# A two-layer trunk on one core: q's second part over zeros, slots moved, last squares added to the fold

## The chip, the cores and the metric

The kernel runs on one core of a Trainium2 chip. A core has TensorE (PE) for matrix products, fed by its own weight loads (PEld), VectorE (DVE), ScalarE (ACT), GpSimd (POOL), SyncE (SP) and 16 DMA engines that they share. The metric is the time of one execution on the device, in microseconds. Before the change it is 965.36 us, the median of three runs (965.27 to 965.42).

## What is computed

A trunk of two layers for 256 tokens of width 1024, in float32. Each layer adds half an FFN, a mixer, and half an FFN, each on a normed input; a last norm follows. The mixer of layer 0 has eight attention heads of width 64, where the three dilated windows come down to one causal score matrix with a fixed mask, and beside them four groups of a spatial gate. The mixer of layer 1 is causal attention with 16 heads of width 64 (with 256 tokens there is one block of 256, so no past block is chosen).

```python
def swiglu(x, w_gate, w_up, w_down):
    return (jax.nn.silu(x @ w_gate) * (x @ w_up)) @ w_down
...
    for layer in range(DEPTH):
        h = h + 0.5 * swiglu(rms_norm(h, ffn1_norm[layer]), ...)
        hn = rms_norm(h, mix_norm[layer])
        if layer % 2 == 0:
            h = h + ab_mixer(hn, ...)
        else:
            h = h + c_mixer(hn, ...)
        h = h + 0.5 * swiglu(rms_norm(h, ffn2_norm[layer]), ...)
    return rms_norm(h, final_norm)
```

In a head: scores are q times k over 64, masked, softmax by rows, then times v.

## The kernel before

Every float32 product is made of three products of rounded parts: each operand is split into a first part, rounded to the format that TensorE takes at full rate (`F32R`), and a second part, the rest. `mm3` (L224 to L226) adds first x first, first x second and second x first. Splitting is an ACT copy that rounds and a DVE subtraction; for the weights these are L105 and L106, elsewhere L229 and L230.

The weights come as a stream of 1 MB tiles: SP loads them into three raw buffers, ACT and DVE split them, and four split buffers are ahead of TensorE. The activations lie transposed, with the width on the 128 partitions, so that a projection tile is 24 products of 128x128 weights by 256 columns (`tile_of`). Two heads of 64 make one tile of 128 partitions, a pair.

Scores need only 64 rows a head. To have q first x (k first + k second) in one product, the 128 rows hold the head's k first on its own half and k second on the other half (`put_k`, tiles k0 and k1), and q first twice (`put_q`, tile q). The remaining product, q second x k first, has the 64 rows of the head alone (`kh` and `ql[r]`, L665). So in `scores` a product with 128 rows (L664) and one with 64 rows (L665) take turns, twice for each head. `put_q` rounds the pair to q1 on ACT, subtracts on DVE into ql, and copies q1 four times on POOL. `put_k` rounds on ACT and subtracts on POOL (L651, L652). In the first mixer put_q and put_k first scale the bank by the norm's row (`scaled`, tile qk); in the second, `rows=True`, only put_k does.

After the scores, DVE adds the mask and takes the row extreme (L668), ACT makes the exponentials (L671), DVE the reciprocal (L674), ACT (first mixer, L678) or POOL (second, L680) scales. `turn` transposes the probabilities on TensorE (L688) and splits them into pth and ptl; `weighted` multiplies them by v and splits the result into mix, which `project` uses.

Around the projection tiles, `Slots` counts a step after each tile (24 products, 8 x 3 in `project`), and calls what is listed for that step: scores, turn, weighted, in the first mixer also mixing (the spatial products L829, which need vn, the normed gate, and wsT) and turn_spatial. That list sets where TensorE does this work; on each of the other engines the framework's scheduler fixes an order when the program is built, and each engine runs its list in that order. Only the first stage has an order written by hand.

The norm's sums are collected as the residual is finished: `Next.pair` is called for four pairs of tiles, squares each on ACT (L279) and adds it on DVE to acc (L283, 128x512). `sums`, later in the next stage, folds acc's two halves into one (L287, 128x256), has TensorE sum over partitions (L290, tile ones), and POOL takes the root (L233). `spread` turns that root to a row through TensorE (L308).

The tiles of a mixer live in a pool that takes the memory of the FFN before it.

Of the kernel before, what the change touches and what calls it, by code (L numbers as in the profile page):

```python
# [10 lines left out]
F32 = mybir.dt.float32  # L11
F32R = mybir.dt.float32r
AF = mybir.ActivationFunctionType
ALU = mybir.AluOpType

S = 256
# [15 lines left out]
LINE, SHIFT = 64, 16  # L32
# [110 lines left out]
def trunk(ctx: ExitStack, tc: tile.TileContext, a, out):  # L143
    nc = tc.nc
# [11 lines left out]
    def bank():  # L156
        return ps.tile([128, 512], F32, name="bank")
# [65 lines left out]
    def mm3(p, sh, sl, mh, ml, start, stop):  # L223
        nc.tensor.matmul(p, sh, mh, start=start, stop=False)  # L224
        nc.tensor.matmul(p, sh, ml, start=False, stop=False)  # L225
        nc.tensor.matmul(p, sl, mh, start=False, stop=stop)  # L226

    def split(hi, lo, src):
        nc.scalar.activation(hi, src, AF.Copy)  # L229
        nc.vector.tensor_sub(lo, src, hi.bitcast(F32))  # L230
# [8 lines left out]
    def both(t):  # L239
        return t.rearrange("p (j s) -> p j s", j=2)  # L240

    def twice(v):
        return v.unsqueeze(1).to_broadcast([128, 2, S])

    class Next:
# [19 lines left out]
        def pair(self, i, p, row=None, pool=None):  # L265

            xs = X[:, 2 * i : 2 * i + 2, :]
            if row is None:
                nc.vector.tensor_add(xs, both(p), xs)
            else:  # L270
                t = pool.tile([128, 2, S], F32, name="part")
                nc.vector.tensor_mul(t, both(p), twice(row))
                nc.vector.tensor_add(xs, t, xs)
            for k in (2 * i, 2 * i + 1):
                self.hi(k, X[:, k])
            for k in (2 * i, 2 * i + 1):
                self.lo(k, X[:, k])
            q = wk.tile([128, 2, S], F32, name="sq" if i else "acc", bufs=1)
            nc.scalar.activation(q, xs, AF.Square, scale=1.0 / math.sqrt(D))  # L279
            if i == 0:  # L280
                self.acc = q
            else:
                nc.vector.tensor_add(self.acc, self.acc, q)  # L283

        def sums(self):
            f = self.acc[:, 0]
            nc.vector.tensor_add(f, f, self.acc[:, 1])  # L287
            p = bank()
            for t in range(NT):
                nc.tensor.matmul(p[:, t : t + 1], f[:, t * 128 : (t + 1) * 128], ones[:, :1], start=True, stop=True)  # L290
            m = wk.tile([128, NT], F32, name="ms")
            nc.vector.tensor_scalar(m, p[:, :NT], EPS, None, op0=ALU.add)  # L292
            self.root(m)
# [322 lines left out]
    def make_attention(mp, mask_cols, nheads, v, mix, engine, rows=False):  # L616

        qs, ks, probs, pts = {}, {}, {}, {}
        pairs, flying = (4, 5) if rows else (3, 4)
        mask = mp.tile([128, 384], F32, name="mask")  # L620
        nc.scalar.dma_start(mask, a["consts"][:, mask_cols])

        def scaled(bk):
            t = mp.tile([128, S], F32, name="qk", bufs=pairs - 1)
            nc.vector.tensor_mul(t, bk[:, :S], norm["row"])
            return t

        def sides(j):
            return slice(j * 64, j * 64 + 64), slice(64 - j * 64, 128 - j * 64)

        def put_q(p, bk):

            t = bk[:, :S] if rows else scaled(bk)
            q1 = mp.tile([128, S], F32R, name="q1", bufs=2)
            ql = mp.tile([128, S + LINE], F32R, name="ql", bufs=pairs)[:, SHIFT : SHIFT + S]
            qq = mp.tile([128, 2 * S + LINE], F32R, name="q", bufs=pairs)
            split(q1, ql, t)
            for j in range(2):
                q = qq[:, SHIFT + j * S : SHIFT + (j + 1) * S]
                r, o = sides(j)  # L640
                for to in (r, o):
                    nc.gpsimd.tensor_copy(q[to, :], q1[r, :].bitcast(F32))  # L642
                qs[2 * p + j] = (q, ql[r, :])

        def put_k(p, bk):

            t = scaled(bk)
            for j in range(2):
                k = mp.tile([128, S], F32R, name=f"k{j}", bufs=pairs)
                r, o = sides(j)  # L650
                nc.scalar.activation(k[r, :], t[r, :], AF.Copy)  # L651
                nc.gpsimd.tensor_sub(k[o, :], t[r, :], k[r, :].bitcast(F32))  # L652
                ks[2 * p + j] = (k, k[r, :])

        def scores(h):
            q, ql = qs.pop(h)
            k, kh = ks.pop(h)
            sc = bank()
            pr = mp.tile([128, 384], F32, name="pr", bufs=flying)
            nm = wk.tile([128, 2], F32, name="nm")  # L660
            l = wk.tile([128, 2], F32, name="l")
            for b in range(2):
                bs = slice(b * 128, b * 128 + 128)
                nc.tensor.matmul(sc[:, b * S : (b + 1) * S], q[:, bs], k, start=True, stop=False)  # L664
                nc.tensor.matmul(sc[:, b * S : (b + 1) * S], ql[:, bs], kh, start=False, stop=True)  # L665
            for b, (c0, n) in enumerate(((0, 128), (128, 256))):
                cs = slice(c0, c0 + n)
                nc.vector.tensor_tensor_reduce(pr[:, cs], sc[:, b * S : b * S + n], mask[:, cs],  # L668
                                               norm["score"][:, b : b + 1] if rows else -SCALE, 3e38,
                                               op0=ALU.add, op1=ALU.min, accum_out=nm[:, b : b + 1])  # L670
                nc.scalar.activation(pr[:, cs], pr[:, cs], AF.Exp, bias=nm[:, b : b + 1], scale=-1.0,  # L671
                                     accum_out=l[:, b : b + 1])
            rl = wk.tile([128, 2], F32, name="rl")
            nc.vector.reciprocal(rl, l)  # L674
            for b, (c0, n) in enumerate(((0, 128), (128, 256))):
                cs = slice(c0, c0 + n)
                if engine is nc.scalar:
                    nc.scalar.activation(pr[:, cs], pr[:, cs], AF.Copy, scale=rl[:, b : b + 1])  # L678
                else:
                    engine.tensor_scalar(pr[:, cs], pr[:, cs], rl[:, b : b + 1], None, op0=ALU.mult)  # L680
            probs[h] = pr

        def turn(h):
            p, j = divmod(h, 2)
            pr = probs.pop(h)
            tp = bank()
            for i in range(3):
                nc.tensor.transpose(tp[:, i * 128 : (i + 1) * 128], pr[:, i * 128 : (i + 1) * 128], ident)  # L688
            if j == 0:
                pts[p] = [mp.tile([128, 2, 384], F32R, name=n, bufs=2) for n in ("pth", "ptl")]  # L690
            split(pts[p][0][:, j, :], pts[p][1][:, j, :], tp[:, :384])

        def weighted(p):
            o = bank().rearrange("p (j c) -> p j c", j=2)
            pth, ptl = pts.pop(p)
            vs = slice(p * 128, (p + 1) * 128)
            mm3(o, v[0][:, 0, vs], v[1][:, 0, vs], pth[:, :, :256], ptl[:, :, :256], True, False)
            mm3(o[:, :, 128:], v[0][:, 1, vs], v[1][:, 1, vs], pth[:, :, 256:], ptl[:, :, 256:], False, True)
            for j in range(2):
                r = slice(j * 64, j * 64 + 64)  # L700
                split(mix[0][r, p], mix[1][r, p], o[r, j, :].rearrange("p (t c) -> p t c", t=NT))

        return put_q, put_k, scores, turn, weighted
# [82 lines left out]
    def ab_mixer(phase):  # L786
        with tc.tile_pool(name="mp", bufs=1) as mp:
# [4 lines left out]
            put_q, put_k, scores, turn, weighted = make_attention(mp, slice(0, 384), 8, v, mix, nc.scalar)  # L792
# [9 lines left out]
            def turn_spatial():  # L802
                pw = bank()
                for g in range(4):
                    nc.tensor.transpose(pw[:, g * 128 : (g + 1) * 128], wsp[:, g, :], ident)
                nc.vector.tensor_copy(wsT, pw.rearrange("p (g c) -> p g c", g=4))
                nc.gpsimd.affine_select(wsT, wsT, pattern=[[0, 4], [1, 128]], compare_op=ALU.is_ge, fill=0.0,
                                        base=0, channel_multiplier=-1)
# [28 lines left out]

            slots = Slots()
            slots.at((9,), lambda _: turn_spatial())
            slots.at((14, 15, 16, 17), mixing)  # L840
            slots.at((5, 6, 7, 8, 20, 20, 21, 21), scores)
            slots.at((8, 9, 10, 11, 22, 22, 23, 23), turn)
            slots.at((11, 13, 24, 25), weighted)

            def put_u(i, p):
                nc.vector.tensor_mul(uT[:, i, :], p[:, :S], norm["row"])
# [81 lines left out]
```

## Time and profile before

| | |
|---|---|
| median of three runs | 965.36 us |
| the profiled execution | 965.54 us |
| its span, first to last instruction | 963.8 us |
| mean granted clock of TensorE | 0.998 |
| first mixer, about | 190 to 290 us |
| second mixer, about | 652 to 774 us |

A group of the profile reads: line, engine, operation, out <- in by the program's names, partitions x elements, count | busy time in us, mean ns of one | idle time of the engine before them, and what ended it. A row of the timeline reads: start in us, duration in us, engine, line, operation, tiles, count of merged instructions, and in brackets the idle time before it with what ended it. PE rows are products, PEld rows their weight loads; both run as a pipeline, so that the duration of one is longer than the distance to the next. Lines of `split` and `mm3` are those of the helper, so the tile's name tells whose they are.

### The profile page before, as it was taken

Reading aid. Unit: us, or ns where it says so; the run is one execution under the profiler, and the core shown is the slowest. Engines: PE = TensorE matmul, PEld = TensorE weight load, DVE = VectorE, ACT = ScalarE, POOL = GpSimd, SP = SyncE. Lnnn points to the kernel's source line nnn. Section 1 sums busy time; section 2 is a strip of 40 time slices with the busy share of each in tenths; the row PEclk is TensorE's granted clock in tenths of the full one; section 3 lists DMA queues with packets and bytes.
Section 4 is the critical chain, followed back from the end, with each engine's and each line's share of the span. In section 5 each row is a group of like instructions: output and inputs, shape, how many; then the busy total and the mean of one; then the engine's idle time right before and its main releaser. Section 6 shows DMA issues by size and latency. Waiting matters only on the chain.

```text
span 963.8 us, 18092 instructions
## 1 busy us (share of the span) xinstructions
PE 952.8 (99%) x7679; PEld 916.9 (95%) x7679; DVE 599.3 (62%) x848; ACT 502.2 (52%) x789; POOL 88.2 (9%) x122
## 2 busy tenths in 40 slices
PE   9999999999999999999999999999999999999997
PEld 8999999978999999999999999998979999999886
DVE  6866556656867665655666565656767676566543
ACT  7744445457675544444454453446666566454431
POOL 0000000030400000000000000004665200000000
PEclk9999999999999999999999999999999999999999
DMA  9865555655445656556666665565434465565521
GB/s 295 276 205 187 186 186 178 218 193 175 132 132 181 208 181 204 180 175 205 202 195 199 185 197 169 193 219 184 139 125 131 132 198 179 181 210 179 208 96 44
DMA packets 153537, 174.86 MB, mean 181 GB/s; under 512 B 3008, under 2 KB 142192, under 8 KB 153456
## 3 DMA queue, kind: packets, MB, share of 16 engines
q1 hardware_dynamic: 151888, 171.54, 55.8%
q10 hardware_dynamic: 1568, 2.17, 0.7%
q8 instruction: 60, 0.98, 0.4%
q14 instruction: 21, 0.17, 0.0%
HBM read 172.65 MB, written 1.05 MB: 180 GB/s over the span
## 4 chain that ended last, share of the span: by engine, by line
PE 94%; DVE 2%; issue 1%; ACT 1%; DMA 1%; POOL 0%; SPq 0%; POOLq 0%
PE bank L224 28%; PE bank L225 28%; PE bank L226 28%; PE bank L539 2%; PE bank L542 2%; PE bank L538 2%; PE bank L665 2%; DVE wlo L106 1%; PE bank L664 1%; PE bank L688 1%; DMA raw<-in_ffn_w_gate 1%; DVE xTl L262 0%; ACT whi L105 0%; DVE acc L283 0%; POOL q L642 0%
## 5 line engine op out<-in xcount | busy, mean ns | idle before, releaser
L105 ACT ACTIVATE whi<-raw 128x1024 fp32r<-128x1024 f32 (+4 forms) x350 | 331.3, 990 | 382.6 <-issue 290.3
L106 DVE TENSOR_TENSOR wlo<-raw,whi 128x1024 fp32r<-128x1024 f32 (+4 forms) x350 | 390.1, 1147 | 140.7 <-ACT whi L105 139.9
L224 PE MATMUL bank<-xTh,whi 128*128 128x256 f32 x1632 | 453.2, 278 | 0.8 <-ACT whi L105 0.8
L225 PE MATMUL bank<-xTl,whi 128*128 128x256 f32 x1632 | 452.0, 277 | 0.1
L226 PE MATMUL bank<-xTh,wlo 128*128 128x256 f32 x1632 | 451.5, 277 | 0.2 <-DVE wlo L106 0.2
L224 PEld LDWEIGHTS bank<-xTh,whi 128*128 128x128 f32 x1632 | 306.4, 188 | 1.4 <-ACT whi L105 1.0
L225 PEld LDWEIGHTS bank<-xTl,whi 128*128 128x128 f32 x1632 | 306.5, 188 | 0.8 <-DVE xTl L262 0.7
L226 PEld LDWEIGHTS bank<-xTh,wlo 128*128 128x128 f32 x1632 | 306.7, 188 | 0.6 <-DVE wlo L106 0.6
L225 PE MATMUL bank<-hTl,whi 128*128 128x256 f32 x528 | 145.9, 276 | 0.0
L226 PE MATMUL bank<-hTh,wlo 128*128 128x256 f32 x528 | 145.8, 276 | 0.0
L224 PE MATMUL bank<-hTh,whi 128*128 128x256 f32 x528 | 145.8, 276 | 0.0
L226 PEld LDWEIGHTS bank<-hTh,wlo 128*128 128x128 f32 x528 | 99.1, 188 | 0.0
L224 PEld LDWEIGHTS bank<-hTh,whi 128*128 128x128 f32 x528 | 99.1, 188 | 0.0
L225 PEld LDWEIGHTS bank<-hTl,whi 128*128 128x128 f32 x528 | 99.1, 188 | 0.0
L481 DVE TENSOR_TENSOR hm<-gs,bank 128x512 f32<-128x512 f32 x44 | 30.1, 687 | 80.5 <-PE bank L226 80.2
L478 DVE TENSOR_TENSOR gs<-bank,row 128x512 f32<-128x512 f32 x44 | 30.0, 689 | 47.5 <-PE bank L226 47.5
L642 POOL CAST q<-q 64x256 fp32r<-64x256 f32 x48 | 27.9, 580 | 198.3 <-ACT q L229 196.7
L233 POOL TENSOR_TENSOR rstd<-ms,half_neg 128x2 f32<-128x2 f32 x6 | 5.1, 849 | 436.7 <-DVE ms L292 419.9
L224 PE MATMUL bank<-mixh,whi 128*128 128x256 f32 x128 | 35.6, 284 | 0.0
L225 PE MATMUL bank<-mixl,whi 128*128 128x256 f32 x128 | 35.3, 280 | 0.0
L226 PE MATMUL bank<-mixh,wlo 128*128 128x256 f32 x128 | 35.1, 278 | 0.0
L230 DVE TENSOR_TENSOR hTl<-hm,hTh 128x512 fp32r<-128x512 f32 x44 | 30.2, 686 | 2.1 <-ACT hTh L229 2.1
(134 smaller groups left out, 877.4 us busy)
## 6 DMA issues: line engine op xcount, KB each, us to landing
raw<-in_ffn_w_gate SPq DMA_DIRECT2D x42, 1024.0 KB, 5.4
raw<-in_ffn_w_up SPq DMA_DIRECT2D x42, 1024.0 KB, 5.4
raw<-in_ffn_w_down SPq DMA_DIRECT2D x35, 1024.0 KB, 5.1
raw<-in_c_w_in SPq DMA_DIRECT2D x12, 1024.0 KB, 5.2
raw<-in_ab_w_in SPq DMA_DIRECT2D x10, 1024.0 KB, 5.1
raw<-in_ffn_w_down SPq DMA_DIRECT2D x12, 768.0 KB, 4.5
raw<-in_ab_w_out SPq DMA_DIRECT2D x4, 1024.0 KB, 5.0
raw<-in_c_w_out SPq DMA_DIRECT2D x4, 1024.0 KB, 4.9
```

Source lines behind the costliest of these rows:

```text
L105: nc.scalar.activation(hi, r, AF.Copy)
L106: nc.vector.tensor_sub(lo, r, hi.bitcast(F32))
L224: nc.tensor.matmul(p, sh, mh, start=start, stop=False)
L225: nc.tensor.matmul(p, sh, ml, start=False, stop=False)
L226: nc.tensor.matmul(p, sl, mh, start=False, stop=stop)
L230: nc.vector.tensor_sub(lo, src, hi.bitcast(F32))
L478: nc.vector.tensor_mul(g, both(pg), twice(norm["row"]))
L481: nc.vector.tensor_mul(hm, g, both(pu))
L538: nc.tensor.matmul(banks[t, h], sh, w[0][kw][:, cs], start=k == 0, stop=False)
L539: nc.tensor.matmul(banks[t, h], sh, w[1][kw][:, cs], start=False, stop=False)
L542: nc.tensor.matmul(banks[t, h], sl, w[0][kw][:, cs], start=False, stop=k == FT - 1)
L642: nc.gpsimd.tensor_copy(q[to, :], q1[r, :].bitcast(F32))
```

## The change

- In `make_attention`, a set of tiles (`seconds`) is made once for a mixer, one for each pair in flight, two halves of 256 columns in each. In the half of head j, the 64 rows of the other head are filled with zeros (POOL, from a tile of zeros). `put_q` writes q's second part to the head's own 64 rows only, and rounds and copies head by head: two ACT copies of 64x256, two DVE subtractions of 64x256 and two POOL copies of 64x256 for a pair, where there were one of 128x256, one of 128x256 and four of 64x256.
- Both score products take 128 rows: the second one multiplies the tile with the zeros by the whole k tile.
- In the first mixer two pairs are in flight instead of three (`pairs`), and the buffers of `qk` are three in both mixers (they were two in the first).
- In the first mixer the first four scores, their turns and the four spatial products come a slot later; the first two weighted sums come at 13 and 14, not 11 and 13. The later slots are as before.
- In `Next.pair`, acc is folded when the third pair has been added, and the last pair's square is added to the folded half in two additions of 128x256. `sums` no longer folds.

On POOL the zero fill, a memset of 128x256 and four copies of 64x256 (eight in the second mixer), stands ahead of the root of the mixer's norm. On ACT, DVE and POOL the order at the mixers shifts with the moved slots: in the first mixer the last spatial group's work on DVE now stands between the keys of the third and of the fourth pair. TensorE's order differs only by the moved slots and by two products of a later tile that come a few places earlier or later. SP's order is the same.

```diff
--- before.py
+++ after.py
@@ -279,12 +279,17 @@
             nc.scalar.activation(q, xs, AF.Square, scale=1.0 / math.sqrt(D))
             if i == 0:
                 self.acc = q
-            else:
+            elif i < 3:
                 nc.vector.tensor_add(self.acc, self.acc, q)
+            f = self.acc[:, 0]
+            if i == 2:
+                nc.vector.tensor_add(f, f, self.acc[:, 1])
+            if i == 3:
+                for j in range(2):
+                    nc.vector.tensor_add(f, f, q[:, j])
 
         def sums(self):
             f = self.acc[:, 0]
-            nc.vector.tensor_add(f, f, self.acc[:, 1])
             p = bank()
             for t in range(NT):
                 nc.tensor.matmul(p[:, t : t + 1], f[:, t * 128 : (t + 1) * 128], ones[:, :1], start=True, stop=True)
@@ -616,12 +621,19 @@
     def make_attention(mp, mask_cols, nheads, v, mix, engine, rows=False):
 
         qs, ks, probs, pts = {}, {}, {}, {}
-        pairs, flying = (4, 5) if rows else (3, 4)
+        pairs, flying = (4, 5) if rows else (2, 4)
+        zeros = mp.tile([128, S], F32, name="zeros")
+        nc.gpsimd.memset(zeros, 0.0)
+        seconds = [mp.tile([128, 2 * S + LINE], F32R, name=f"ql{i}") for i in range(pairs)]
+        for t in seconds:
+            for j in range(2):
+                o = slice(64 - j * 64, 128 - j * 64)
+                nc.gpsimd.tensor_copy(t[o, SHIFT + j * S : SHIFT + (j + 1) * S], zeros[o, :])
         mask = mp.tile([128, 384], F32, name="mask")
         nc.scalar.dma_start(mask, a["consts"][:, mask_cols])
 
         def scaled(bk):
-            t = mp.tile([128, S], F32, name="qk", bufs=pairs - 1)
+            t = mp.tile([128, S], F32, name="qk", bufs=3)
             nc.vector.tensor_mul(t, bk[:, :S], norm["row"])
             return t
 
@@ -631,16 +643,14 @@
         def put_q(p, bk):
 
             t = bk[:, :S] if rows else scaled(bk)
-            q1 = mp.tile([128, S], F32R, name="q1", bufs=2)
-            ql = mp.tile([128, S + LINE], F32R, name="ql", bufs=pairs)[:, SHIFT : SHIFT + S]
             qq = mp.tile([128, 2 * S + LINE], F32R, name="q", bufs=pairs)
-            split(q1, ql, t)
             for j in range(2):
-                q = qq[:, SHIFT + j * S : SHIFT + (j + 1) * S]
+                q, ql = (u[:, SHIFT + j * S : SHIFT + (j + 1) * S] for u in (qq, seconds[p % pairs]))
                 r, o = sides(j)
-                for to in (r, o):
-                    nc.gpsimd.tensor_copy(q[to, :], q1[r, :].bitcast(F32))
-                qs[2 * p + j] = (q, ql[r, :])
+                nc.scalar.activation(q[r, :], t[r, :], AF.Copy)
+                nc.vector.tensor_sub(ql[r, :], t[r, :], q[r, :].bitcast(F32))
+                nc.gpsimd.tensor_copy(q[o, :], q[r, :].bitcast(F32))
+                qs[2 * p + j] = (q, ql)
 
         def put_k(p, bk):
 
@@ -650,11 +660,11 @@
                 r, o = sides(j)
                 nc.scalar.activation(k[r, :], t[r, :], AF.Copy)
                 nc.gpsimd.tensor_sub(k[o, :], t[r, :], k[r, :].bitcast(F32))
-                ks[2 * p + j] = (k, k[r, :])
+                ks[2 * p + j] = k
 
         def scores(h):
             q, ql = qs.pop(h)
-            k, kh = ks.pop(h)
+            k = ks.pop(h)
             sc = bank()
             pr = mp.tile([128, 384], F32, name="pr", bufs=flying)
             nm = wk.tile([128, 2], F32, name="nm")
@@ -662,7 +672,7 @@
             for b in range(2):
                 bs = slice(b * 128, b * 128 + 128)
                 nc.tensor.matmul(sc[:, b * S : (b + 1) * S], q[:, bs], k, start=True, stop=False)
-                nc.tensor.matmul(sc[:, b * S : (b + 1) * S], ql[:, bs], kh, start=False, stop=True)
+                nc.tensor.matmul(sc[:, b * S : (b + 1) * S], ql[:, bs], k, start=False, stop=True)
             for b, (c0, n) in enumerate(((0, 128), (128, 256))):
                 cs = slice(c0, c0 + n)
                 nc.vector.tensor_tensor_reduce(pr[:, cs], sc[:, b * S : b * S + n], mask[:, cs],
@@ -837,10 +847,10 @@
 
             slots = Slots()
             slots.at((9,), lambda _: turn_spatial())
-            slots.at((14, 15, 16, 17), mixing)
-            slots.at((5, 6, 7, 8, 20, 20, 21, 21), scores)
-            slots.at((8, 9, 10, 11, 22, 22, 23, 23), turn)
-            slots.at((11, 13, 24, 25), weighted)
+            slots.at((15, 16, 17, 18), mixing)
+            slots.at((6, 7, 8, 9, 20, 20, 21, 21), scores)
+            slots.at((9, 10, 11, 12, 22, 22, 23, 23), turn)
+            slots.at((13, 14, 24, 25), weighted)
 
             def put_u(i, p):
                 nc.vector.tensor_mul(uT[:, i, :], p[:, :S], norm["row"])
```

## The prediction

> **What bounds the kernel now.** I read the head of the profile page first (busy time, the chain of work that ended last, the granted clock), then the groups of instructions with shapes kept apart, then the waits of TensorE, then the timeline around the score products.
>
> ```profile
> span 963.8 us, 18092 instructions
> PE 952.8 (99%) x7679; PEld 916.9 (95%) x7679; DVE 599.3 (62%) x848; ACT 502.2 (52%) x789; POOL 88.2 (9%) x122
> PEclk9999999999999999999999999999999999999999
> PE 94%; DVE 2%; issue 1%; ACT 1%; DMA 1%; POOL 0%; SPq 0%; POOLq 0%
> ...
> L665 PE MATMUL bank<-k,ql 64*128 64x256 f32 x48 | 18.3, 381 | 0.0
> L664 PE MATMUL bank<-k,q 128*128 128x256 f32 x48 | 16.4, 343 | 0.9 <-POOL k L652 0.9
> ```
>
> TensorE is busy for 99% of the span at the full clock, and the chain that ends last is TensorE for 94%. So time can only be taken out by giving TensorE less work or by making its products follow each other faster. The two score products stand out: 381 and 343 ns, though they have 256 columns like nearly all others. A duration in a pipelined engine is not its cost; the cost is the distance from one start to the next. For a plain product with 256 columns and for one with 512 that distance is:
>
> ```profile
> 653.83 0.28 PE L226 MATMUL bank<-xTh,wlo 128*128 128x256 f32 x1
> 653.94 0.28 PE L224 MATMUL bank<-xTh,whi 128*128 128x256 f32 x1
> 653.94 0.19 PEld L225 LDWEIGHTS bank<-xTl,whi 128*128 128x128 f32 x1
> 654.05 0.28 PE L225 MATMUL bank<-xTl,whi 128*128 128x256 f32 x1
> 654.17 0.28 PE L226 MATMUL bank<-xTh,wlo 128*128 128x256 f32 x1
> ...
> 212.30 0.39 PE L225 MATMUL bank<-wlo,xTh 128*128 128x512 f32 x1
> 212.53 0.39 PE L226 MATMUL bank<-whi,xTl 128*128 128x512 f32 x1
> ```
>
> From 653.83 to 654.17 are three steps: 0.113 us each for 256 columns; with 512 columns 0.23. The weight load takes 0.19 us, more than the step, so it runs beside the product before it. Now one head's four score products and what follows them, and below it the first and last row of two heads in a row (eight score products and one product with 512 columns between the two starts):
>
> ```profile
> 212.75 0.28 PE L664 MATMUL bank<-k,q 128*128 128x256 f32 x1
> 212.96 0.38 PE L665 MATMUL bank<-k,ql 64*128 64x256 f32 x1
> 213.27 0.39 PE L664 MATMUL bank<-k,q 128*128 128x256 f32 x1
> 213.59 0.38 PE L665 MATMUL bank<-k,ql 64*128 64x256 f32 x1
> 213.90 0.51 PE L224 MATMUL bank<-whi,xTh 128*128 128x512 f32 x1
> 214.24 0.40 PE L225 MATMUL bank<-wlo,xTh 128*128 128x512 f32 x1
> ...
> 745.15 0.28 PE L664 MATMUL bank<-k,q 128*128 128x256 f32 x1
> ...
> 747.88 0.39 PE L225 MATMUL bank<-ptl,vth 128*128 128x512 f32 x1
> ```
>
> One head: 212.75 to 214.24 is 1.49 us, where 4 x 0.113 + 0.23 = 0.68 would do: 0.81 us too much. Two heads: 2.73 us against 8 x 0.113 + 0.23 = 1.13, 1.60 too much. Every step between a product with 128 rows and one with 64 costs 0.2 to 0.31 us instead of 0.11, and the step after the last one as well. Steps between products that all have 128 rows cost nothing extra, whatever tiles they read.
>
> **The change, part by part.**
>
> (a) Both score products on 128 rows. L665's weights become a tile with q's second part on the head's half and zeros on the other, and its moving side the whole k tile. The instruction count stays, 96 products, and the row change is gone. If a score product then steps like the plain ones above, a head saves 0.80 us: 24 heads, 19.2 us, all of it on TensorE's path. From below: if they stay as they are, nothing. I take 0.80, because L664 with the same q and k tiles takes its normal place as long as its neighbours have 128 rows (it starts 0.22 after the row at 212.53).
>
> The Trainium skill, page TensorEngine Tiling (Array Packing), section Tiling Modes, says that a change of tiling mode drains TensorE; the steps of 0.31 us agree with that, and by it the whole 19.2 us go.
>
> (b) The scalar, vector and GpSimd work for q. A pair has two ACT copies of 64x256 instead of one of 128x256, two DVE subtractions for one, and two POOL copies for four.
>
> ```profile
> L642 POOL CAST q<-q 64x256 fp32r<-64x256 f32 x48 | 27.9, 580 | 198.3 <-ACT q L229 196.7
> L230 DVE TENSOR_TENSOR mixl<-bank,mixh 64x256 fp32r<-64x256 f32 x24 | 10.0, 418 | 5.7 <-ACT mixh L229 5.6
> L229 ACT ACTIVATE mixh<-bank 64x256 fp32r<-64x256 f32 x24 | 9.0, 376 | 12.1 <-DVE mixl L230 9.5 <-PE bank L226 2.5
> ```
>
> The nearest rows of 64x256 are 376 ns (ACT) and 418 ns (DVE): 12 pairs add 4.5 us on ACT and 5.0 on DVE and take 24 x 0.58 = 14 us off POOL. ACT and DVE are 52% and 62% busy, so it hides under TensorE except where they are full (d). Without that cover it is 0.8 us a pair at most.
>
> (c) Waits that the moved slots and the fold take away.
>
> ```profile
> PE bank L829 <- DVE vn L823: 1.0, 1, 1.0
> PE bank L664 <- POOL k L652: 0.9, 1, 0.9
> ...
> PE bank L290 <- DVE acc L287: 0.4, 2, 0.2
> ```
>
> The first score waits 0.9 us for k; a slot of 24 products (24 x 0.113 = 2.7 us) later k is there. The spatial products wait 1.0 us for vn; again 2.7 us later. The sums wait 0.4 us for the fold, which stood behind a weight split on DVE; now one 128x256 addition is done a pair earlier and two finish the sum. Together 2.3 us at most. Whether the 1.0 us stays saved is part of (d).
>
> (d) What comes late next: the end of the first mixer. There the scores of heads 4 to 7, their turns and the last weighted sums follow close on each other, and two engines are full:
>
> ```profile
> 245.00:261.00 16.00, 16.00 (x143) 16.00 (x142) 14.40 (x30) 7.95 (x15) 5.72 (x9) 1.00 0.42 135
> 261.00:283.00 22.00, 22.00 (x159) 19.71 (x158) 13.09 (x33) 17.95 (x42) 4.50 (x4) 1.00 0.56 170
> ...
> 272.72 1.49 ACT L678 ACTIVATE pr<-pr,rl 128x128 f32<-128x128 f32 x4
> 274.24 0.87 ACT L229 ACTIVATE pth<-bank 128x384 fp32r<-128x384 f32 x2
> 276.08 2.01 ACT L105 ACTIVATE whi<-raw 128x1024 fp32r<-128x1024 f32 x2 [0.97 <-PE bank L225]
> 278.00 0.85 ACT L229 ACTIVATE pth<-bank 128x384 fp32r<-128x384 f32 x2
> 279.45 1.02 DVE L230 TENSOR_TENSOR ptl<-bank,pth 128x384 fp32r<-128x384 f32 x2
> ...
> 280.74 0.39 PE L225 MATMUL bank<-ptl,vth 128*128 128x512 f32 x1
> ```
>
> The columns of the first two rows are PE, PEld, DVE, ACT and POOL busy. DVE is busy for 14.4 of 16 us before the last keys are ready, and ACT for 17.95 of 22 after them. The order there keeps the same splits and exponentials and adds the fourth spatial product behind the third pair's key. So measured from the end of the gate's token block, DVE and ACT reach heads 4 to 7 no earlier than now, though TensorE could be 0.8 x 4 + 1.0 = 4.2 us earlier. ACT ends the last scaling at 274.2. Behind it stand pth (0.87), two splits (2.01) and pth (0.85), the only idle time in it being 0.97: that is what can be gained, 278.85 becomes about 277.9. The product that reads ptl starts at 280.74, 0.27 after ptl's end at 280.47, so TensorE gains 0.97 + 0.27 = 1.2 us at this place instead of 4.2. Bounds: 0 (DVE later still) and 4.2 (the queues move along). I take 1.2.
>
> (e) The end of the second mixer, where POOL scales.
>
> ```profile
> 758.68 1.50 POOL L680 TENSOR_SCALAR pr<-pr,rl 128x128 f32<-128x128 f32 x2 [1.24 <-DVE rl L674]
> 760.22 0.81 PE L688 MATMUL bank<-ident,pr 128*128 128x128 f32 x6
> ```
>
> The last head's probabilities end at 760.18 and its three transposes, the second half of the six, start 0.33 after the first: 0.37 us of room. Between that pair's scores and these transposes TensorE loses 1.6 us, but the chain begins that much earlier too and has to pass the same queues. I take 0.3 us lost, bounds 0 and 1.5.
>
> (f) The zero fill. It stands on POOL ahead of the norm's root: one memset and eight copies in the second mixer (four in the first).
>
> ```profile
> 652.49 0.69 DVE L273 TENSOR_TENSOR x<-part,x 128x512 f32<-128x512 f32 x1
> 658.44 0.70 POOL L233 TENSOR_TENSOR rstd<-ms,half_neg 128x2 f32<-128x2 f32 x1
> 663.41 0.38 PE L308 MATMUL bank<-ident,wide 128*128 128x128 f32 x2
> ```
>
> The space belongs to the FFN until 653.2. Nine operations of 0.58 us end by 658.4, when the root starts now; its result is needed on TensorE at 663.41. Cost 0.
>
> The sum: heads 0 to 3 3.2, first score 0.9, end of the first mixer 1.2, 16 heads of the second 12.8, fold 0.4, less 0.3: 18.2 us. Span 963.8 - 18.2 = 945.6. The profiled execution took 965.5, 1.7 above its span and 0.2 above the median, so 947.1 us.
>
> **The rivals.**
>
> Nothing is lost again: the queues of ACT and DVE move along with TensorE in both mixers. For it: both have idle time on the whole. Against it: the two windows in (d). Time: 965.4 - 19.2 - 2.3 = 943.9.
>
> More is lost: both mixers' ends give back all that their last four heads save (3.2 each, and the 1.0), and the fill is late for the root. Time: 947.1 + 1.2 + 2.9 = 951.2; with a fill at three times my durations, 15.7 us from 653.2, the root ends at 669.6 instead of 659.1, 6 us past the transposes at 663.41: 957. Against it: POOL's mean is 0.58.
>
> The change does not do what it says: loads to all 128 rows are exposed, and a step costs a load and a product, 0.19 + 0.11 = 0.30, as the 0.31 now. Then the score products save nothing, and the first score's 0.9 and the fold's 0.4 remain, with 0.3 of the 1.0: 963.8. Against it: the rows from 653.83 to 654.17, where loads of 0.19 hide in steps of 0.113. The Trainium skill, TensorE: Matmul & The Clock Gate, part 3, section The mechanism, says that a weight load overlaps products in flight only where the row groups differ; that speaks against this change, and it is what this rival would be. The rows at 653.94 disagree with it, load and product start together on the same 128 rows.
>
> Slower: the clock. More of the array works, and the throttle answers. All of TensorE's 952.8 us scale with the clock, so every 1% costs 9.5 us, and it decides from 1.9% below full (18.2 / 952.8); at 2.5% below, 971. Against it: the clock row is 9 in every slice, and nearly all products have 128 rows now.
>
> **How the numbers follow.** The forecast, 947.1, has 0.70; nothing lost 0.14; more lost 0.10; no saving 0.03; slower 0.03. The range runs from 943.7, just under the rival without losses, to 951.3, where both ends are lost. A measurement of this kernel cannot tell less than about 0.2% (1.9 us) from no change: no saving at 963.8 lies within it. Faster 0.94, same 0.03, slower 0.03.
>
> **What would show it.** Steps of 0.11 us between the score products, and a duration of both near 278 ns (a); if they stay at 0.31, the main term falls. No wait of the first score for k, of the spatial products for vn, of the sums for acc (c). New waits of TensorE for pr or ptl, or for k, between 255 and 280 us, of about 3 us in all (d), and at most 1 us in the second mixer's end (e). The root on POOL no later than now against the mixer's first product (f). I am wrong if the score products keep their distance, or if new waits in the mixers pass 7 us.

## The result, and the profile after

| | before | after |
|---|---|---|
| median | 965.39 us | 951.42 us (948.47, 948.53, 954.32, 954.40) |
| the profiled execution, its span | 965.54, 963.8 us | 948.47, 946.7 us |
| mean granted clock | 0.998 | 0.999 |

The ratio is 0.9853, with a 95% interval of 0.9809 to 0.9896: the kernel became faster by about 14 us. The forecast was 947.1. The times after the change fall into two groups, near 948.5 and near 954.4, and no execution lies at the median; the profile shown here is of the lower group, and comparisons below are made within one group (the groups differ in one stage; the last section has it).

The head of the page, and the groups of the two score products:

```profile
span 946.7 us, 18120 instructions
PE 935.5 (99%) x7679; PEld 911.8 (96%) x7679; DVE 607.1 (64%) x865; ACT 506.8 (54%) x801; POOL 87.0 (9%) x112
PEclk9999999999999999999999999999999999999999
...
L674 PE MATMUL bank<-k,q 128*128 128x256 f32 x48 | 12.4, 285 | 0.9 <-POOL k L662 0.9
L675 PE MATMUL bank<-k,ql 128*128 128x256 f32 x48 | 12.1, 279 | 0.0
```

The instruction count of TensorE is the same and its busy time is 17.3 us shorter. The score products last 285 and 279 ns, about as long as the others with 256 columns. The timeline of TensorE around one head:

```profile
213.90 0.28 PE L674 MATMUL bank<-k,q 128*128 128x256 f32 x1
214.02 0.28 PE L675 MATMUL bank<-k,ql 128*128 128x256 f32 x1
214.14 0.28 PE L674 MATMUL bank<-k,q 128*128 128x256 f32 x1
214.26 0.28 PE L675 MATMUL bank<-k,ql 128*128 128x256 f32 x1
214.38 0.40 PE L224 MATMUL bank<-whi,xTh 128*128 128x512 f32 x1
214.61 0.40 PE L225 MATMUL bank<-wlo,xTh 128*128 128x512 f32 x1
```

The steps between them are 0.12 us, and the head with the product behind it takes 0.71 us where it took 1.49. That is 0.78 us a head. What TensorE waits for now (total, times, longest):

```profile
PE bank L295 <- DVE acc L289: 1.4, 2, 0.8
...
PE bank L674 <- POOL k L662: 0.9, 2, 0.7
PE bank L225 <- DVE ptl L230: 0.7, 1, 0.7
...
PE bank L698 <- POOL pr L690: 0.2, 1, 0.2
```

No wait for vn is left. The sums (L295) wait for acc longer than before, 1.4 us instead of 0.4. Where the time came from can be read at two marks, the residual's last addition (L273) before the second mixer and the last row of TensorE. The second one was, before:

```profile
957.14 0.28 PE L226 MATMUL bank<-whi,hTl 128*128 128x256 f32 x1
```

and both are now:

```profile
646.96 0.69 DVE L273 TENSOR_TENSOR x<-part,x 128x512 f32<-128x512 f32 x1
...
940.05 0.28 PE L226 MATMUL bank<-whi,hTl 128*128 128x256 f32 x1
```

The addition started at 652.49 before: 5.5 us gained in and around the first mixer. The last row is 17.1 us earlier, so 11.6 us were gained in the second mixer and behind it. The working of the prediction gave 5.5 (3.2 + 0.9 + 1.2 + 0.2) for the first and 12.7 (12.8 + 0.2 - 0.3) for the second. What is missing, 1.1 us, is in the second mixer, and most of it ahead of its first head: TensorE's step to the first product of the sums is 1.06 us there, where it was 0.49. There the DVE of before went, around the fold of the norm's squares:

```profile
654.23 0.88 DVE L262 SCALAR_TENSOR_TENSOR xTl<-x,gT,xTh 128x256 fp32r<-128x256 f32 x2
655.07 0.69 DVE L283 TENSOR_TENSOR acc<-acc,sq 128x512 f32<-128x512 f32 x1
655.68 1.22 DVE L106 TENSOR_TENSOR wlo<-raw,whi 128x1024 fp32r<-128x1024 f32 x1
656.81 0.42 DVE L287 TENSOR_TENSOR acc<-acc 128x256 f32<-128x256 f32 x1
```

and the DVE, POOL and PE of after go:

```profile
648.71 1.16 DVE L262 SCALAR_TENSOR_TENSOR xTl<-x,gT,xTh 128x256 fp32r<-128x256 f32 x2
649.79 0.62 DVE L289 TENSOR_TENSOR acc<-acc,sq 128x256 f32<-128x256 f32 x1
650.33 1.41 DVE L106 TENSOR_TENSOR wlo<-raw,whi 128x1024 fp32r<-128x1024 f32 x1
651.66 0.62 DVE L289 TENSOR_TENSOR acc<-acc,sq 128x256 f32<-128x256 f32 x1
652.20 0.41 DVE L651 TENSOR_TENSOR ql<-bank,q 64x256 fp32r<-64x256 f32 x1
...
648.23 5.19 POOL L631 CAST ql<-zeros 64x256 fp32r<-64x256 f32 x8
...
652.42 0.58 PE L295 MATMUL bank<-ones,acc 128*128 128x1 f32 x4 [0.79 <-DVE acc L289]
```

As long as POOL copies zeros, from 648.23 to 653.42, each addition and the split are about 0.2 us longer (0.62 for 0.42, 1.41 for 1.22) and the two xTl together 0.28; L651 is not, with 0.41. So the prediction's "Cost 0" for the fill left something out.

### The profile page after: what moved, and what is told of

Its sections match the earlier page's. It is cut to its first block, busy times and chain, and to the rows that moved or that the text cites. A ratio compares the mean times of both kernels' runs of the same rounds, so it can differ in the third digit from the quotient of the medians.

```text
span 946.7 us, 18120 instructions
## 1 busy us (share of the span) xinstructions
PE 935.5 (99%) x7679; PEld 911.8 (96%) x7679; DVE 607.1 (64%) x865; ACT 506.8 (54%) x801; POOL 87.0 (9%) x112
## 4 chain that ended last, share of the span: by engine, by line
PE 66%; DVE 4%; ACT 3%; issue 1%; POOL 0%; POOLq 0%; ACTq 0%
PE bank L225 20%; PE bank L224 20%; PE bank L226 20%; DVE wlo L106 2%; PE bank L544 2%; PE bank L547 2%; PE bank L543 2%; ACT whi L105 1%; ACT pr L681 1%; PE bank L698 0%; DVE xTl L262 0%; PE bank L674 0%; PE bank L675 0%; DVE mixl L230 0%; ACT pr L688 0%
## 5 line engine op out<-in xcount | busy, mean ns | idle before, releaser
L690 POOL TENSOR_SCALAR pr<-pr,rl 128x128 f32<-128x128 f32 (+1 forms) x32 | 30.2, 955 | 15.4 <-DVE rl L684 15.1
```

## Experiments

Times are in microseconds. The lower and the upper group of times are compared separately.

**The changed kernel again** ("again", no edit), beside the runs that follow.

> The changed kernel once more, because its four times stood in two pairs, 948.5 and 954.4 us. If the second pair belongs to the chip or the moment, all times of this call lie near one of the two values, and the kernel before moves with them (966.5 went with one pair, 965.3 with the other). If it belongs to the kernel itself, both values come up within this call.

Measured: 948.47 and 948.57, and 954.34 to 955.23 four times; ratio 0.9863 (0.9837 to 0.9888). With the first four, four of ten executions are in the lower group. The executions of before beside these lie from 964.61 to 966.84, in one group.

**The padding alone** ("pad_only"): the kernel of before with the tiles over zeros and both products on 128 rows, its slots and its fold unchanged. (q's head-by-head split, the two pairs in flight and the three buffers of `qk` come with it.)

```diff
         def scores(h):
...
-                nc.tensor.matmul(sc[:, b * S : (b + 1) * S], ql[:, bs], kh, start=False, stop=True)
+                nc.tensor.matmul(sc[:, b * S : (b + 1) * S], ql[:, bs], k, start=False, stop=True)
```

> Parts (a) and (b) alone: 128 rows for both score products, with the slots and the fold of before. Theory (the row change costs): steps of 0.11 us between score products, the fold's wait back at 0.4 us in all, the wait of the spatial products for vn back at about 1 us, and the end of the first mixer bound by ACT and DVE as in the changed kernel: 948 to 951 us, that is 5 us or less from the changed kernel. Rival (the moved slots and the fold bring it): 960 us or more.

**The changed kernel with the fold of before** ("old_fold"):

```diff
-            elif i < 3:
+            else:
                 nc.vector.tensor_add(self.acc, self.acc, q)
...
         def sums(self):
             f = self.acc[:, 0]
+            nc.vector.tensor_add(f, f, self.acc[:, 1])
```

> The changed kernel with the fold of before. In the changed kernel the sums' first product starts 0.75 and 0.95 us late at the two mixers, before 0.38 each; theory: the second addition of the new fold has a weight split ahead of it on DVE, so undoing it gives back about 0.9 us: 0.9 us less than the changed kernel on the same chip. Rival (the fold is neutral, the late start is due to the shorter chain elsewhere): no difference within 0.3 us.

Measured: the padding alone 949.43 and 949.95, upper group 956.24 to 956.83; with the slots too (the fold of before) 948.49 and 949.23, upper group 954.45 to 955.36. Ratios 0.9882 (0.9857 to 0.9908) and 0.9869 (0.9845 to 0.9892). So the padding makes nearly all of the gain, about 15.6 us (965.3 - 949.7), and the slots add 0.8 us in the lower group and about 1.5 in the upper one. The waits of TensorE in "pad_only" say where:

```profile
PE bank L290 <- DVE acc L287: 1.9, 2, 1.1
PE bank L834 <- DVE vn L828: 1.4, 1, 1.4
```

The wait of the spatial products for vn is there (L834) and is 0 with the new slots. And the sums wait 1.9 us, against 0.4 before the change and 1.4 with both the fill and the new fold: the padding made the sums late, and the new fold takes back only part of it. The theory for "old_fold", that undoing the new fold gives back 0.9 us, was wrong: its lower times are not below those of "again" (948.47 and 948.57).

**The row change alone** ("grouped"): the kernel of before, with the two products of 128 rows of a head first and the two of 64 rows behind them. It isolates the step at a change of rows.

```diff
-            for b in range(2):
-                bs = slice(b * 128, b * 128 + 128)
-                nc.tensor.matmul(sc[:, b * S : (b + 1) * S], q[:, bs], k, start=True, stop=False)
-                nc.tensor.matmul(sc[:, b * S : (b + 1) * S], ql[:, bs], kh, start=False, stop=True)
+            for u, to, last in ((q, k, False), (ql, kh, True)):
+                for b in range(2):
+                    bs = slice(b * 128, b * 128 + 128)
+                    nc.tensor.matmul(sc[:, b * S : (b + 1) * S], u[:, bs], to, start=not last and b == 0, stop=last and b == 1)
```

> The kernel before, with the score products of a head in another order: both with 128 rows, then both with 64. Theory (the change of the row count costs): two changes a head instead of four, so about 24 x 0.4 = 9.6 us less than before, 955 to 957 us. Rival (a product with 64 rows is slow by itself): as before, 965 us.

Measured: 955.04 to 955.61 (four runs), ratio 0.9894 (0.9881 to 0.9906), as the theory had it. One head in its timeline:

```profile
211.72 0.40 PE L665 MATMUL bank<-k,q 128*128 128x256 f32 x2
212.05 0.50 PE L665 MATMUL bank<-k,ql 64*128 64x256 f32 x2
212.48 0.50 PE L224 MATMUL bank<-whi,xTh 128*128 128x512 f32 x1
212.82 0.39 PE L225 MATMUL bank<-wlo,xTh 128*128 128x512 f32 x1
```

From 211.72 to 212.82 are 1.10 us where 0.68 would do: 0.42 too much, half of the 0.81 of the alternating order. The same four products, with fewer changes of rows between them, cost half as much: it is the change that costs, not the narrow product in itself.

**The fill made late** ("late_fill"): the same copies, but the tile of zeros is made from the norm's root, so that they start behind the sums. The first copies of q and the root come first on POOL.

```diff
-        nc.gpsimd.memset(zeros, 0.0)
...
+        def fill():
+            nc.gpsimd.tensor_scalar(zeros, X[:, 0, :], norm["col"][:, 0:1], 0.0, op0=ALU.mult, op1=ALU.mult)
...
         nxt.sums()
+        nxt.fill()
```

> The changed kernel with the zero fill on POOL made to wait for the norm's root. In the changed kernel every DVE operation beside the fill is 0.2 us longer (0.88 to 1.16 for two xTl, 1.22 to 1.41 for a split, 0.42 to 0.62 for the fold) and the sums start 0.75 and 0.95 us late. Theory (the fill on POOL slows DVE): the durations return to those of before and the sums start at most 0.4 us late at both mixers, about 1 us less from the FFN's last product to the mixer's end. Rival (DVE's order alone makes the sums late): the durations and the late start stay as they are.

Measured: 946.89, 946.95 and 947.43, upper group 953.58 to 955.01; ratio 0.9845 (0.9816 to 0.9874). The lower group is 1.4 us below that of the changed kernel. TensorE's waits have no line for acc any more, and DVE has its old durations (the traced execution is the one of 955.01, so its rows start later):

```profile
656.67 0.42 DVE L289 TENSOR_TENSOR acc<-acc,sq 128x256 f32<-128x256 f32 x1
657.02 1.22 DVE L106 TENSOR_TENSOR wlo<-raw,whi 128x1024 fp32r<-128x1024 f32 x1
658.15 0.42 DVE L289 TENSOR_TENSOR acc<-acc,sq 128x256 f32<-128x256 f32 x1
```

So the copies beside these operations made the sums late. Whether any work of POOL does that, or only work that reads, this run doesn't tell.

**A fill that only writes** ("memset_fill"): eight memsets straight into the halves, at the place of the copies.

```diff
-        zeros = mp.tile([128, S], F32, name="zeros")
-        nc.gpsimd.memset(zeros, 0.0)
...
-                nc.gpsimd.tensor_copy(t[o, SHIFT + j * S : SHIFT + (j + 1) * S], zeros[o, :])
+                nc.gpsimd.memset(t[o, SHIFT + j * S : SHIFT + (j + 1) * S].bitcast(F32), 0.0)
```

> The changed kernel, with the zeros written by eight memsets of 64x256 straight into the halves (four in the first mixer) in place of one memset and eight copies; POOL then only writes while it fills and reads nothing. Theory: what slowed VectorE beside the fill is that both read the memory through one port, so only VectorE operations with both inputs there, beside a GpSimd operation that reads, are longer. Then the square's additions go back from 0.62 to 0.42 us, the weight split from 1.41 to 1.22, the two xTl from 1.16 to 0.88, although the fill stands at the same place; TensorE's sums wait for acc at most 0.4 us in all instead of 1.4, and the lower times are 946.9 to 947.5 (948.5 in the changed kernel). Rival: any GpSimd work beside VectorE slows it, writing too. Then these durations stay longer for as long as the memsets run (8 of about 0.2 to 0.3 us, some 2 us), at least two of the four operations keep 0.2 us more, the sums still wait 0.8 us or more in all, and the lower times are 947.8 to 948.5. Second rival: the additions are longer because of what they read (ACT's squares just written); then nothing changes.

Measured: 946.35, 946.40, 946.49, 946.52 and 947.24; no execution in an upper group; ratio 0.9775 (0.974 to 0.981), beside executions of before that ran from 965.32 to 967.73, and three from 971.91 to 973.61. DVE and POOL at the same place:

```profile
647.58 0.88 DVE L262 SCALAR_TENSOR_TENSOR xTl<-x,gT,xTh 128x256 fp32r<-128x256 f32 x2
648.42 0.43 DVE L289 TENSOR_TENSOR acc<-acc,sq 128x256 f32<-128x256 f32 x1
648.76 1.22 DVE L106 TENSOR_TENSOR wlo<-raw,whi 128x1024 fp32r<-128x1024 f32 x1
...
646.81 2.72 POOL L629 MEMSET ql<- 64x256 f32 x8 [169.81 <-DVE x L273]
...
650.46 0.58 PE L295 MATMUL bank<-ones,acc 128*128 128x1 f32 x4
```

The memsets run from 646.81 to 649.53, beside the xTl, an addition and the start of the split, and these have their undisturbed durations to 0.01 us. The sums don't wait. Theory right, both rivals wrong: it is the reading of POOL beside DVE that slows DVE. This version beats both kernels: 946.5 stands against 948.5 for the lower group of the changed kernel and 965.4 for the median of before. Row by row, 1.5 of the 2.0 us stand at the two sums (the steps to their first products are 0.22 us instead of 0.86 and 1.06).

**The fold of before with that fill** ("memset_old_fold"): the fill of memsets, with the fold of before.

> The same memset fill, with the fold of before (three additions of 128x512, then one of 128x256 in the sums). It gives the worth of the new fold alone, with VectorE undisturbed. Theory: the sums wait 0.4 us in all, as before the change, since nothing runs beside VectorE that reads; so the new fold is worth at most 0.4 us (0 to 0.4 in the lower times: 947.0 to 947.9). Rival: the new fold is what makes up for the fill; then without it the sums wait about 1 us at each mixer as in the run with the fold of before and the copies, and the lower times are 948.5 to 949.2.

Measured: 947.71 to 948.21, and 953.87 once; ratio 0.9799 (0.9766 to 0.9832). The sums wait 0.4 us in all, the theory's number:

```profile
PE bank L290 <- DVE acc L287: 0.4, 2, 0.2
```

The times are 1.5 us above those of "memset_fill" (948.03 against 946.49, the middle ones of the lower groups), more than the 0.4 that the wait shows and that the theory allowed; neither the theory nor its rival has that number. Laid row by row, the two traced executions (946.52 and 947.71) part by 0.27 us at the first sums and about as much at the second, together some 0.5. Another 0.4 arises between 288 and 297 us, where TensorE waits for nothing but gets through 77 products instead of 81; the last section comes back to such stretches.

**Three tries at what is left.** First the scaling of the first mixer on POOL ("pool_scale"), which takes work off ACT where the prediction had it full:

```diff
-            put_q, put_k, scores, turn, weighted = make_attention(mp, slice(0, 384), 8, v, mix, nc.scalar)
+            put_q, put_k, scores, turn, weighted = make_attention(mp, slice(0, 384), 8, v, mix, nc.gpsimd)
```

> The changed kernel with the first mixer's probabilities scaled on POOL, as in the second mixer. Theory (ACT's queue sets the end of the first mixer): the waits of TensorE for pr and ptl between 260 and 280 us, 1.5 us together with the step behind them, shrink to 0.5 us or less, the two for k (1.2 us) stay; about 1 us less in that stage. Rival (it is DVE's queue, or POOL is slower): the waits stay or grow.

Then the fourth spatial product a slot later ("mix19"), which takes DVE's work for it away from between the last keys:

```diff
-            slots.at((15, 16, 17, 18), mixing)
+            slots.at((15, 16, 17, 19), mixing)
```

> The changed kernel with the fourth spatial product a slot later still, behind both last keys. Theory (its work on DVE between the two keys makes the keys late): the two waits for k, 0.8 and 0.4 us, fall to 0.3 us or less; of the 1.2 us about half comes out at the end, as ACT binds behind it. Rival (the keys are late through the splits ahead of them on DVE): the first wait stays at 0.8 us.

And one tile more with tokens on the partitions in the second FFN of layer 0 ("reset5"), against the upper group of times:

```diff
-    add_ffn(a["ffn2_w_gate"][0], a["ffn2_w_up"][0], a["ffn2_w_down"][0])
+    add_ffn(a["ffn2_w_gate"][0], a["ffn2_w_up"][0], a["ffn2_w_down"][0], again=(2, 3, 5))
```

> The changed kernel with one more tile of the second FFN's weights laid out in the other way (the third up tile). The two times of the changed kernel, 948.5 and 954.4, differ by one stage: in the second FFN each step is 113.3 ns in one execution and 117.8 in the other, from the transposes after the first mixer's sums to the next interruption. Theory (the step length is a state, set where the stream of products is interrupted, and the other layout sends it to the short one): all times at 948 to 950 us, none near 954. Rival (the other layout has no hold on it): two groups as before, 6 us apart.

"pool_scale" took 949.55 to 952.72, ratio 0.985 (0.9836 to 0.9864), all above the lower group of the changed kernel. The wait for ptl is gone, and the transposes wait for POOL instead:

```profile
PE bank L698 <- POOL pr L690: 2.7, 3, 1.3
```

"mix19" took 948.82 to 949.74 and 955.56 once, ratio 0.9831 (0.9816 to 0.9845): no gain. Its waits (in the execution of 955.56):

```profile
PE bank L698 <- ACT pr L688: 0.7, 1, 0.7
PE bank L674 <- POOL k L662: 0.5, 1, 0.5
```

The keys come earlier (0.5 us of waiting for 0.9), and the transposes then wait 0.7 us for ACT's scaling, which the changed kernel didn't. In both tries what one queue gave the next one took, and neither theory held.

"reset5" took 948.66, and 953.51 to 954.58 four times, ratio 0.9868 (0.9849 to 0.9887): both groups remain, so the theory behind it fell.

## Why the prediction was right

The profiled execution, 948.5, lies in the range (943.7 to 951.3), 1.4 us above the forecast. The median, 951.42, is 4.3 us above it and 0.1 beyond the end of the range; 2.9 of the 4.3 come from the upper group, which no step of the prediction had. That the median is no further off is luck: it hangs on how many executions fall into that group, two of four here and four of six in "again", whose median is 954.37.

**(a), the score products: right.** A head gains 0.78 us (0.80 predicted), 18.7 us for 24 heads. "pad_only" shows that this part carries the result, and "grouped" that the cost hangs on the number of row changes: with four, two and none a head loses 0.81, 0.42 and 0.03 us. The Trainium skill, page TensorEngine Tiling (Array Packing), section Tiling Modes, which has TensorE drained at a change of mode, agrees with all three kernels. The other rule weighed, that loads overlap only where row groups differ (the Trainium skill, page TensorE: Matmul & The Clock Gate, part 3, section The mechanism), doesn't hold here: the steps are 0.12 us with loads of 0.19 on the same 128 rows.

**(b), q's extra operations: right,** as far as TensorE's waits show: none of them is for q or ql. DVE has 17 operations more (those of the fold among them) and ACT 12, and they are busy 7.8 and 4.6 us longer.

**(c), the waits: right for the first score and for vn, wrong in sign for the sums.** The prediction gained 0.4 at the sums. Their waits grew by 1.0 us (1.4 for 0.4); (f) has the reason.

**(d), the end of the first mixer: right in size.** The prediction had about 3 us of new waits for k, pr and ptl between 255 and 280 us. In the timeline of after:

```profile
257.58 0.39 PE L674 MATMUL bank<-k,q 128*128 128x256 f32 x1 [0.66 <-POOL k L662]
...
258.53 0.38 PE L674 MATMUL bank<-k,q 128*128 128x256 f32 x1 [0.21 <-POOL k L662]
...
269.02 1.51 PE L698 MATMUL bank<-ident,pr 128*128 128x128 f32 x6
...
275.27 0.51 PE L225 MATMUL bank<-ptl,vth 128*128 128x512 f32 x1 [0.69 <-DVE ptl L230]
```

The delays beyond normal steps are 0.82 and 0.38 us at the keys, 0.86 at ptl and 0.56 within the transposes at 269 (six of them take 1.51 us): 2.6 us in all. (The brackets are smaller, since they count only time in which no product is in flight.) The split among them was not predicted, and the two tries on it show that DVE, POOL and ACT take turns there: freeing one of them exposes another. That the first mixer gives just the 5.5 us of the forecast is in part luck: its sums came 0.4 us later where 0.2 of gain stood, and the end, with 2.6 lost for 3.0, gave most of that back.

**(e), the end of the second mixer: right,** 0.3 us lost as said, at the second half of the transposes, which waits for POOL's pr (at 743.49, a step of 0.45 us for 0.11). With it the second mixer's account closes: 16 x 0.78 less 0.57 at the sums and 0.34 here is the 11.6 us of the marks.

**(f), the fill, is the step that failed: "Cost 0".** The prediction asked whether the fill makes the root late, and priced it with 0.58 us an operation (the copies took 0.65). There it was right in the cost: the root does start 0.5 us later against the first product of the sums than before (1.53 us behind it for 1.06), which the prediction's sign ruled out, but TensorE's transposes of the root wait for nothing. It didn't ask what POOL does to the engine beside it. That made the sums late, which (c) had gain. The rows for it stood in the trace of before. There POOL copies q from 256.05 to 259.67, and DVE goes, first without POOL and then beside it:

```profile
250.42 0.42 DVE L835 TENSOR_TENSOR tmp<-tmp,uT 128x256 f32<-128x256 f32 x1
250.76 1.22 DVE L106 TENSOR_TENSOR wlo<-raw,whi 128x1024 fp32r<-128x1024 f32 x1
...
256.05 3.62 POOL L642 CAST q<-q 64x256 fp32r<-64x256 f32 x4 [0.65 <-ACT q L229]
...
257.46 0.61 DVE L835 TENSOR_TENSOR tmp<-tmp,uT 128x256 f32<-128x256 f32 x1
257.99 1.41 DVE L106 TENSOR_TENSOR wlo<-raw,whi 128x1024 fp32r<-128x1024 f32 x1
```

The same 0.2 us. In the second mixer the two xTl, the first addition, the split and the last addition came out 0.28, 0.20, 0.19 and 0.20 us longer, 0.87 in all. Less the 0.27 that the new fold saves there (an addition of 0.42 for one of 0.69) this is 0.60, and the sums came 0.57 later; counted with the fill, these rows would have turned the gain at the sums into the loss that came. Without it, the lower times of "memset_fill" and "late_fill" (946.4 to 947.4) are where the forecast stood.

**The rivals.** Nothing lost fell by (d), more lost by the second mixer's end, no saving by the steps, and slower by the clock, 0.999.

## What to carry to other kernels

Where products of 64 and of 128 rows take turns, zeros that fill the narrow one up to 128 rows can be cheaper than the narrow product: 0.78 us for four products here; if that can't be done, put products of the same rows together, for half of it. Before work that looks free is put on an idle engine, look in the trace for the busy engine's durations with and without it, not only for whether its own result is in time. And a filling of zeros is better written than copied.

## What the runs showed of the hardware

**POOL's reads slow DVE, its writes don't.** A DVE operation with both inputs in SBUF takes about 0.2 us longer beside POOL's copies (0.62 for 0.42, 1.41 for 1.22), and nothing more beside POOL's memsets. One whose first input is a bank of TensorE's results, L651 at 652.20, keeps its 0.41 beside the copies. The Trainium skill, page SBUF — State Buffer, section Who interferes with whom, states just this: a vector instruction with two SBUF inputs contends with a GpSimd instruction that reads SBUF, not with one that only writes it. The trace agrees with the condition. The same page of the Trainium skill also has, in its section Summary: rules for kernel authors, the second of the two wait until the first is done. Two single copies of the changed kernel agree with that on POOL's side:

```profile
650.71 1.30 POOL L631 CAST ql<-zeros 64x256 fp32r<-64x256 f32 x1
...
653.47 0.40 POOL L652 CAST q<-q 64x256 fp32r<-64x256 f32 x1
```

The first starts within the split that runs from 650.33 to 651.74, and ends only behind it, at 652.01. The second, of the same size, has no such operation beside it. DVE's delay is about 0.2 us for operations of 0.42 and of 1.22 alike; that would fit a wait for what is left of one copy in progress, but it was not tested with copies of another size.

**TensorE has two step lengths for the same products.** The two groups of times differ in one stage, the second FFN of layer 0. In the window 310 to 400 us of the changed kernel (948.47, first row) and of "again" (954.34, second), with the columns PE busy and products, clock, DMA share and GB/s:

```profile
310.00:400.00 90.00, 90.00 (x796) 1.00 0.59 187
```

```profile
310.00:400.00 90.00, 90.00 (x766) 1.00 0.58 184
```

At the same clock of 1.00, 90 us hold 796 products in the one and 766 in the other: about 113 and 118 ns each. From the transposes of this stage's root to the next sums (302.07 to 476.65 in the one, 301.34 to 482.53 in the other) that makes 6.6 us; the second execution came to the stage 0.7 us earlier, so 5.9 is left, the distance of the groups. From 500 to 600 us both executions run at 113 ns again. The profiled executions at 954.34, 955.01 ("late_fill") and 955.56 ("mix19") have 766 or 767 products in the window, all others, that of before among them, 795 to 797. TensorE is busy for all of the window in each of them. Short stretches of the long step stand in other stages too: from 295.6 to 301.3 us in the kernel of before, from 290.1 to 295.8 in the changed one, from 289.7 to 295.4 in "memset_old_fold", and no such stretch in "memset_fill" and "grouped". So in the three traced executions of the upper group such a stretch lasts through a whole stage. What chooses the length is open: an extra tile of the other layout ("reset5") didn't remove the upper group. Beside "memset_fill" the kernel of before, too, has three of eleven executions some 6 us above the rest (971.91 to 973.61). There is no trace of them, so whether they have the long step is not shown; if they have, the change did not bring it.
